# Attention scores over 64 queries of two heads and 192 keys instead of 128 queries of one head and 256 keys

## The chip, the cores and the metric

The kernel runs on one core of a Trainium2 chip. The metric is the device time of one execution in microseconds. A core has a matrix engine (TensorE, "PE" in the profile, with its weight loads as "PEld"), VectorE ("DVE"), ScalarE ("ACT"), GpSimd ("POOL") and SyncE ("SP"), which issues most of the DMAs. Each engine works through its own instructions in order, and semaphores tie the engines together.

## What is computed

One layer of a decoder trunk over 2048 tokens of width 1024, in float32. The input is modulated, u is multiplied with a wide weight matrix, and the result is cut into queries, keys, values, gates and the input of a causal pool. The part that matters here is attention in a window of 128 keys, with 16 query heads of 64 dimensions that share 2 key heads, a bias by distance and one sink logit for each head:

```python
mask = in_window & key_exists            # dist = q_loc + 128 - k_loc, 0 <= dist < 128
logits = einsum('bnqhgd,bnkhd->bnhgqk', qb, kb) * HEAD_DIM ** -0.5 + bias
logits = where(mask, logits, NEG_INF)
probs = softmax(concatenate([logits, sink], -1))[..., :-1]
out = einsum('bnhgqk,bnkhd->bnqhgd', probs, vb)
```

A block of 128 queries meets 256 keys: its own block and the one before. A query at place i of the block sees only the keys i + 1 to i + 128 of these 256. So the first 64 queries of a block see nothing beyond key 191, and the last 64 nothing before key 64.

## The kernel before, in words

Matrices are multiplied as split pairs: each operand is a rounded high part (float32r) and the remainder, and three products (high-high, high-low, low-high) make one. Blocks of four matrices ("quads") are multiplied with seven products instead of eight, after Strassen and Winograd; a product is 12 matmuls of 128x128 weights on 512 columns. The sequence is cut into two halves of 1024 tokens (s = 0, 1). Each half has a start phase, a long phase with 13 single quads in which attention runs beside the products, and an end phase; then come the output phases. `plan` writes the order of products, weight splits and loads ahead of time, and `run` emits them; every operation is kept in program order on its engine. All instructions are recorded by one helper, so the profile gives them all line 56, and they are told apart by tiles.

Attention is the function `overlay`. It has 64 steps a half (8 pairs of heads x 8 blocks of 128 queries). `beat` is called after every three matmuls of a product and now and then emits one `step(n)`, which is software-pipelined over four blocks:

- `scores(n)` on TensorE: four matmuls into the bank `lg`, for each of the two heads one for the high and one for the low part of the keys (tile `kk`); the weights are 128 queries of that head (tile `qs`, high and low parts of the queries one above the other in the 128 rows).
- `transposes(n - 2)`: four 128x128 transposes of the probabilities into the single bank `pt`; `values(n - 3)`: four matmuls into `pv`.
- For step n - 1, VectorE takes the reciprocal of the sums and ScalarE scales the probabilities. ScalarE copies `pt` to `pth` and half of `pv` to `o2`; VectorE later makes the remainder `ptl` and adds the halves into `st`.
- For step n, for each head, VectorE adds the bias tile `bt` to the scores and takes the minimum against the negated sink (one instruction with accumulator), into a tile `L`, and ScalarE takes the exponential with the sum, with the sink as a 257th column.

`L` is a ring of three tiles of 2 x 257 + 4 numbers, and POOL writes the sink columns of the next one (`new_l`). `bt` has one buffer of 2 heads x 256 numbers, reloaded for each pair of heads by `load_bias`. Queries are written to DRAM (`q_d`) by `q_quad` as they are computed, and come back by `load_q` into two buffers of `qs`, two steps at a time. `e_rep` holds the bias rows, repeated for 128 partitions, and `spread_bias` fills it.

A first half's first block has no block before it; its scores are over 128 keys only (`k0_of`).

Score banks: the products of paired quads use the bank `lg` too, and `behind` writes it in full once with a dummy matmul where a phase starts with a fresh bank.

Of the kernel before, what the change touches and what calls it, by code (L numbers as in the profile page):

```python
# [12 lines left out]
F32 = mybir.dt.float32  # L13
F32R = mybir.dt.float32r
# [5 lines left out]
P = 128  # L20
# [39 lines left out]
def kernel(  # L60
# [29 lines left out]

    BF16 = mybir.dt.bfloat16
    set_names = ("B11", "T1", "T2", "B21", "T3", "B22", "T4")

# [53 lines left out]
    def as32(ap):  # L147
        return ap.bitcast(F32)
# [165 lines left out]
    def defer(ticks, f, local=False):  # L314
        due.append((now[0] + ticks, len(due), f, local))
# [136 lines left out]
    def behind(ph, q, kind, h):  # L452
        if kind == "F":
            if h == 0:
                q.c = bank(("lg", "c1")[q.x] if q.pair else "mm")
                if q.x and ph.fresh:
                    t = sets["B11"][:, 0, 0, :]
                    mm(q.c, t[:, 0:P], t, start=True, stop=True, skip_group_check=True)
                    ph.fresh = False
# [88 lines left out]
    def kv_quad(s):  # L548
# [25 lines left out]
        return Quad((win[TK], win[TV]), consume)  # L574

    def q_quad(s, m):
        def consume(ph, mi, t, src):
            hi, lo = ph.c("q_hi", F32R), ph.c("q_lo", F32R)
            act.activation(hi, src, AF.Copy, scale=-0.125)
            dve.scalar_tensor_tensor(lo, src, -0.125, as32(hi), ALU.mult, ALU.subtract)  # L580
            defer(2 if m else 1, lambda: [sp.dma_start(q_d[s, m + mi, t, n], as32(x)) for n, x in enumerate((hi, lo))])
# [184 lines left out]
    def spread_bias(j, q):  # L766
        q.dma_start(e_rep[:, 2 * j : 2 * j + 2, :], e_d[2 * j : 2 * j + 2, :].partition_broadcast(P))

    def overlay(ph, s, n_slots):
# [26 lines left out]
        def load_q(h):  # L796
            if h >= N // 2:
                return
            j, t, c = h // NB, h // 2 % 2, h % 2
            q = qts[h] = tp.tile([P, 2, 2 * P], F32R, tag="qs", bufs=2, name="qs")  # L800
            for n in range(2):
                src = q_d[s, j, t, n][:, c * 2 * P : (c + 1) * 2 * P].rearrange("(h d) c -> d h c", h=2)
                sp.dma_start(as32(q[n * HD : (n + 1) * HD]), src)

        def load_bias(j):
            if j >= KT:
                return
            bt = bts[j] = tp.tile([P, 2, 2 * P], F32, tag="bt", bufs=1, name="bt")
            e_src = e_rep[:, 2 * j : 2 * j + 2, :]
            sp.dma_start(bt, bass.AP(e_src.tensor, e_src.offset + P - 1, [[HEADS * ET - 1, P], [ET, 2], [1, 2 * P]]))  # L810

        def new_l(n):
            if n < N:
                j = n // U
                room = tp.tile([P, 2 * 257 + 4], F32, tag="L", bufs=3, name="L")
                Ls[n] = room[:, 0 : 2 * 257].rearrange("p (h k) -> p h k", h=2)
                marks[n] = room[:, 2 * 257 : 2 * 257 + 2], room[:, 2 * 257 + 2 :]
                pool.tensor_copy(Ls[n][:, :, 256], nsink[:, 2 * j : 2 * j + 2])

# [3 lines left out]
        def values(n):  # L823
            k0 = k0_of(n)
            pv = pvs[n] = bank("pv")[:, 0 : 2 * P].rearrange("p (h q) -> p h q", h=2)
            pair = xs.pop(n)
            todo = [(hf, x) for hf in range(k0 // P, 2) for x in pair]
            for i, (hf, x) in enumerate(todo):
                mm(pv, kvt["v"][:, n % U + hf - 1 + s, :], x[:, hf], start=i == 0, stop=i == len(todo) - 1)

        def scores(n):
            k0, b, q = k0_of(n), n % U, qts[n // 2]
            lg = bank("lg").rearrange("p (h k) -> p h k", h=2)
            at = n % 2 * P
            for h in range(2):
                for hl in range(2):
                    mm(
                        lg[:, h, k0:],
                        q[:, h, at : at + P],
                        kvt["k"][:, hl, (b - 1 + s) * P + k0 : (b + 1 + s) * P],  # L840
                        start=h == 0 and hl == 0,
                        stop=hl == 1,
                        skip_group_check=True,
                    )
            return lg

        def transposes(n):
            L = Ls.pop(n)
            pt = ps.tile([P, 2, 2, P], F32, tag="pt", bufs=1, name="pt")
            for hf in range(k0_of(n) // P, 2):  # L850
                for h in range(2):
                    pe.transpose(pt[:, hf, h, :], L[:, h, hf * P : (hf + 1) * P], ident)
            return pt
# [20 lines left out]
        def step(n):  # L874
# [4 lines left out]
            if n - 1 in Es:  # L879
                E, e0, sm = Es.pop(n - 1)  # L880
                dve.reciprocal(sm, sm)
                for h in range(2):
                    act.activation(E[:, h, e0:256], E[:, h, e0:256], AF.Copy, scale=sm[:, h : h + 1])
            if pt is not None:
# [9 lines left out]
            if lg is not None:  # L894
                j, e0 = n // U, k0_of(n)
                L = Ls[n]
                nm, sm = marks.pop(n)
                for h in range(2):
                    dve.tensor_tensor_reduce(
                        L[:, h, e0:256],  # L900
                        lg[:, h, e0:],
                        bts[j][:, h, e0:],
                        1.0,
                        nsink[:, 2 * j + h : 2 * j + h + 1],
                        ALU.add,
                        ALU.min,
                        nm[:, h : h + 1],
                    )
                    act.activation(
                        L[:, h, e0:257],  # L910
                        L[:, h, e0:257],
                        AF.Exp,
                        bias=nm[:, h : h + 1],
                        scale=-1.0,
                        accum_out=sm[:, h : h + 1],
                    )
                Es[n] = L, e0, sm
            if pt is not None:
                low(dve, lo[:, h0:], pt[:, h0:], hi[:, h0:])
            if o2 is not None:  # L920
# [7 lines left out]
                for h in range(2):  # L928
                    dve.tensor_tensor(
                        outs[jj, tt][h * HD : (h + 1) * HD, bb * P : (bb + 1) * P], pv[0:HD, h, :], o2[:, h, :], ALU.add  # L930
                    )
                if bb == NB - 1:
# [282 lines left out]
    def head(ph, grp):  # L1215
# [402 lines left out]
```

## Time and profile before

| what | value |
|---|---|
| median of three runs | 1698.69 us (1698.04 to 1703.2) |
| the profiled execution | 1703.35 us |
| its span, first to last instruction | 1701.2 us |
| mean granted TensorE clock | 0.993 |
| busy: PE, DVE, ACT, POOL | 98%, 70%, 58%, 35% |
| DMA packets | 236833, 389.50 MB |

The profile is one execution, and its busy shares are of the span. Attention of the first half runs from about 161 to 480 us, that of the second from about 743 to 1060 us. Matmuls are pipelined, so the length of one in the profile is its latency; the time from the start of one to the start of the next tells what it costs in a dense stretch.

### The profile page before, as it was taken

To read this page: it belongs to the slowest core of one execution; us is meant where nothing else is said; L and a number is where in the kernel's file an instruction comes from. 1 tells how busy PE (TensorE), PEld (TensorE's weight loads), DVE (VectorE), ACT (ScalarE), POOL (GpSimd) and SP (SyncE) were. 2 spreads that over 40 slices of the span, in tenths; PEclk is the share of its full clock that TensorE was granted. 3 is DMA by queue.
4 is the path that set the end of the run, shared out by engine and by line. 5 is a ranking of instruction groups with operands and counts; after the bars stand their busy time and mean duration, and the time that the engine had idled before them with its cause. 6 is when DMAs were issued, how large, how long until landed. Compare 5 with 4: busy or idle time off the path is not lost.

```text
span 1701.2 us, 24948 instructions
## 1 busy us (share of the span) xinstructions
PE 1665.3 (98%) x8112; PEld 1397.0 (82%) x8112; DVE 1185.1 (70%) x2167; ACT 988.4 (58%) x1943; POOL 589.4 (35%) x563
## 2 busy tenths in 40 slices
PE   9899999999999999999999999999999999999997
PEld 7788888888788888888888888888888888888886
DVE  6855666666647778656666666487876785778878
ACT  4645888787853336358877787333544453434553
POOL 3013454545462223323424333322242211113544
PEclk9899999999999999999999999999999999999999
DMA  9489676776557889865456454589968685777343
GB/s 358 151 294 311 202 225 217 242 239 208 170 178 223 264 288 326 289 206 157 150 171 215 156 175 135 190 280 326 329 238 309 197 312 201 261 264 281 149 149 124
DMA packets 236833, 389.50 MB, mean 229 GB/s; under 512 B 20872, under 2 KB 90528, under 8 KB 236576
## 3 DMA queue, kind: packets, MB, share of 16 engines
q1 hardware_dynamic: 231280, 382.36, 66.8%
q10 hardware_dynamic: 5392, 5.53, 1.0%
q8 instruction: 64, 1.05, 0.3%
q14 instruction: 65, 0.53, 0.1%
q0 software_dynamic: 32, 0.02, 0.0%
HBM read 243.63 MB, written 147.35 MB: 230 GB/s over the span
## 4 chain that ended last, share of the span: by engine, by line
PE 68%; ACT 11%; DVE 6%; issue 5%; DMA 3%; POOL 1%; SPq 1%; DVEq 0%; ACTq 0%; POOLq 0%
PE mm L56 43%; PE lg L56 11%; PE c L56 9%; ACT L L56 5%; PE pv L56 3%; PE pt L56 3%; DVE w_set L56 2%; ACT pth L56 2%; ACT w_set L56 1%; DVE wide L56 1%; ACT sig L56 1%; DVE p L56 1%; DVE ptl L56 1%; SPq L56 1%; ACT q_hi L56 0%
## 5 line engine op out<-in xcount | busy, mean ns | idle before, releaser
L56 PE MATMUL mm<-set_B,w_set 128*128 128x512 f32 x2664 | 652.7, 391 | 0.6 <-DVE w_set L56 0.6
L56 PEld LDWEIGHTS mm<-set_B,w_set 128*128 128x128 f32 x2664 | 496.6, 188 | 103.7 <-DVE w_set L56 1.5
L56 PE MATMUL mm<-set_T,w_set 128*128 128x512 f32 x1896 | 466.1, 392 | 1.5 <-POOL w_set L56 1.2
L56 POOL TENSOR_TENSOR W<-W 128x512 f32<-128x512 f32 x185 | 266.9, 1453 | 573.1 <-DVE w_set L56 394.0
L56 PEld LDWEIGHTS mm<-set_T,w_set 128*128 128x128 f32 x1896 | 351.5, 189 | 74.4 <-POOL w_set L56 2.5
L56 DVE TENSOR_TENSOR w_set<-W,w_set 128x1024 fp32r<-128x1024 f32 x197 | 254.5, 1292 | 110.5 <-ACT w_set L56 109.2
L56 ACT ACTIVATE L<-L 128x257 f32<-128x257 f32 (+3 forms) x512 | 241.4, 498 | 96.8 <-DVE L L56 96.3
L56 ACT CAST w_set<-W 128x1024 fp32r<-128x1024 f32 x222 | 232.2, 1047 | 97.2 <-PE mm L56 54.2
L56 PE MATMUL lg<-set_T,w_set 128*128 128x512 f32 x828 | 201.0, 391 | 2.7 <-ACT lg L56 1.7
L56 PE MATMUL c<-set_T,w_set 128*128 128x512 f32 x828 | 200.8, 391 | 0.0
L56 PEld LDWEIGHTS lg<-set_T,w_set 128*128 128x128 f32 x828 | 155.4, 188 | 36.2 <-ACT lg L56 2.1
L56 PEld LDWEIGHTS c<-set_T,w_set 128*128 128x128 f32 x828 | 155.8, 189 | 32.2
L56 DVE TENSOR_TENSOR ptl<-pt,pth 128x512 fp32r<-128x512 f32 (+1 forms) x128 | 86.4, 675 | 112.6 <-ACT pth L56 112.6
L56 POOL TENSOR_TENSOR W<-W,A 128x512 f32<-128x512 f32 x41 | 57.9, 1412 | 275.1 <-DMA A<-in_win_dram 102.7
L56 DVE CUSTOM_DVE_ANT_0 L<-lg,bt,nsink 128x256 f32<-128x256 f32 (+1 forms) x256 | 110.1, 467 | 25.1 <-PE lg L56 20.9
L56 ACT ACTIVATE sig<-mm 128x512 f32<-128x512 f32 x76 | 45.5, 599 | 94.6 <-PE mm L56 92.5
L56 PEld LDWEIGHTS lg<-kk,qs 128*128 128x128 f32 x512 | 77.4, 189 | 15.4 <-DVE L L56 4.6
L56 PE MATMUL pt<-ident,L 128*128 128x128 f32 x496 | 76.7, 276 | 9.3 <-DVE ptl L56 8.8
L56 PE MATMUL lg<-kk,qs 128*128 128x256 f32 (+1 forms) x512 | 81.5, 281 | 2.2 <-DVE L L56 1.9
L56 POOL TENSOR_TENSOR w_set<-W,w_set 128x1024 fp32r<-128x1024 f32 x25 | 61.0, 2441 | 63.7 <-ACT w_set L56 37.5
L56 PE MATMUL pv<-pth,vv 128*128 128x256 f32 x248 | 74.8, 323 | 1.1 <-DMA vv<-v_d 1.1
L56 DVE TENSOR_TENSOR st<-pv,o 64x128 f32<-64x128 f32 x256 | 71.3, 279 | 5.5 <-ACT o L56 3.8
(207 smaller groups left out, 1884.2 us busy)
## 6 DMA issues: line engine op xcount, KB each, us to landing
W<-in_win_dram SPq DMA_DIRECT2D x40, 512.0 KB, 5.8
qs<-q_d SPq DMA_DIRECT2D x128, 128.0 KB, 4.3
sums_d<-W SPq DMA_DIRECT2D x62, 256.0 KB, 4.1
W<-sums_d SPq DMA_DIRECT2D x31, 512.0 KB, 4.2
ain_d<-st SPq DMA_DIRECT2D x56, 256.0 KB, 3.5
A<-in_win_dram SPq DMA_DIRECT2D x42, 256.0 KB, 5.6
q_d<-q_hi SPq DMA_DIRECT2D x32, 256.0 KB, 4.4
q_d<-q_lo SPq DMA_DIRECT2D x32, 256.0 KB, 4.2
```

Source lines behind the costliest of these rows:

```text
L56: return lambda *args, **kw: self.tc.keep_in_program_order(op(*args, **kw))
```

## The change

The scores of a step are cut by queries and not by heads. A matmul's weights are now 64 queries of both heads (the first or the last half of the block, index `eo`), and it runs over 192 keys: 0 to 191 for the first half, 64 to 255 for the last. The add-and-minimum, the exponential and the scaling work on the same 192 keys. `L` becomes three standing tiles of 2 x 257 + 14 numbers; the 128 places between the two halves' keys are set to zero once a phase by POOL, so that the transposes still read four 128x128 squares. The sink stands before the keys of the first half and behind those of the last. `bt` holds 64 queries of both heads over 192 places (the bias depends on the distance alone, so both halves share it), has two buffers and takes two DMAs. Queries lie in DRAM in pieces of 64. `nsink` and `sinks` are laid out with the two heads of a pair in the two halves of the partitions. Where an end phase starts, the dummy matmul is done for both banks.

The core of the diff:

```diff
-    nsink = cp.tile([P, HEADS], F32, name="nsink")
+    nsink = cp.tile([P, 2 * KT], F32, name="nsink")[:, :KT]
-    e_rep = dp.tile([P, HEADS, ET], F32, name="e_rep")
+    e_rep = dp.tile([HD, HEADS, ET], F32, name="e_rep")
-    q_d = dp.tile([2, KT, 2, 2, P, CH], F32, name="q_d")
+    q_d = dp.tile([2, KT, 2, 2, CH // HD, P, HD], F32, name="q_d")
...
-            self.fresh = True
+            self.fresh = {0, 1} if "pg" in bufs else {1}
...
-                if q.x and ph.fresh:
+                if q.pair and q.x in ph.fresh:
...
+    def keep_q(dst, x):
+        sp.dma_start(dst.rearrange("b p c -> p b c"), x.rearrange("p (b c) -> p b c", c=HD))
...
+        rooms = [tp.tile([P, 2 * 257 + 14], F32, tag=f"L{i}", bufs=1, name="L") for i in range(3)]
+        for room in rooms:
+            pool.memset(room[:, 1 + BAND : 1 + BAND + P], 0.0)
...
-                src = q_d[s, j, t, n][:, c * 2 * P : (c + 1) * 2 * P].rearrange("(h d) c -> d h c", h=2)
+                src = q_d[s, j, t, n, 4 * c : 4 * c + 4].rearrange("b (h d) c -> d (b h) c", h=2)
...
-            bt = bts[j] = tp.tile([P, 2, 2 * P], F32, tag="bt", bufs=1, name="bt")
+            bt = bts[j] = tp.tile([P, BAND], F32, tag="bt", bufs=2, name="bt")
+            for h in range(2):
...
+        def span_of(n, eo):
+            k0 = k0_of(n)
+            return (max(k0, HD), 2 * P) if eo else (k0, BAND)
...
-            for h in range(2):
+            for eo in range(2):
+                whi = q[:, n % 2 * 2 + eo].rearrange("p h c -> p (h c)")
+                k0, k1 = span_of(n, eo)
                 for hl in range(2):
                     mm(
-                        lg[:, h, k0:],
-                        q[:, h, at : at + P],
-                        kvt["k"][:, hl, (b - 1 + s) * P + k0 : (b + 1 + s) * P],
+                        lg[:, eo, k0:k1],
+                        whi,
+                        kvt["k"][:, hl, (b - 1 + s) * P + k0 : (b - 1 + s) * P + k1],
...
-                    act.activation(E[:, h, e0:256], E[:, h, e0:256], AF.Copy, scale=sm[:, h : h + 1])
+                    x = E[:, 1 + 2 * P * eo + k0 : 1 + 2 * P * eo + k1]
+                    act.activation(x, x, AF.Copy, scale=sm[:, eo : eo + 1])
...
-        act.dma_start(nsink, sinks.partition_broadcast(P))
+        for h in range(2):
+            act.dma_start(nsink[h * HD : (h + 1) * HD, :], sinks[h].partition_broadcast(HD))
...
-        "sinks": a["sinks"][0],
+        "sinks": a["sinks"][0].reshape(-1, 2).T,
```

BAND is 192, P 128, HD 64, KT 8 and CH 512.

More of the change, by code (lines that the diff above doesn't have):

```diff
@@ L580, in consume @@
             dve.scalar_tensor_tensor(lo, src, -0.125, as32(hi), ALU.mult, ALU.subtract)
-            defer(2 if m else 1, lambda: [sp.dma_start(q_d[s, m + mi, t, n], as32(x)) for n, x in enumerate((hi, lo))])
+            defer(2 if m else 1, lambda: [keep_q(q_d[s, m + mi, t, n], as32(x)) for n, x in enumerate((hi, lo))])
         kept = (sums_d[1 + m // 2], s == 1) if m else ()
@@ L847, in transposes @@
         def transposes(n):
-            L = Ls.pop(n)
+            L = Ls.pop(n)[:, 1 : 1 + 4 * P].rearrange("p (e k) -> p e k", e=2)
             pt = ps.tile([P, 2, 2, P], F32, tag="pt", bufs=1, name="pt")
             for hf in range(k0_of(n) // P, 2):
-                for h in range(2):
-                    pe.transpose(pt[:, hf, h, :], L[:, h, hf * P : (hf + 1) * P], ident)
+                for eo in range(2):
+                    pe.transpose(pt[:, hf, eo, :], L[:, eo, hf * P : (hf + 1) * P], ident)
             return pt
@@ L894, in step @@
             if lg is not None:
[L895 to L896 removed]
+                j, L = n // U, Ls[n]
                 nm, sm = marks.pop(n)
[L898 removed]
+                for eo in range(2):
+                    k0, k1 = span_of(n, eo)
+                    a, c = (1 + 2 * P * eo + k for k in (k0, k1))
                     dve.tensor_tensor_reduce(
[L900 to L902 removed]
+                        L[:, a:c],
+                        lg[:, eo, k0:k1],
+                        bts[j][:, k0 - HD * eo : k1 - HD * eo],
                         1.0,
[L904 removed]
+                        nsink[:, j : j + 1],
                         ALU.add,
                         ALU.min,
[L907 removed]
+                        nm[:, eo : eo + 1],
                     )
+                    with_sink = L[:, a : c + 1] if eo else L[:, a - 1 : c]
                     act.activation(
[L910 to L911 removed]
+                        with_sink,
+                        with_sink,
                         AF.Exp,
[L913 removed]
+                        bias=nm[:, eo : eo + 1],
                         scale=-1.0,
[L915 removed]
+                        accum_out=sm[:, eo : eo + 1],
                     )
[L917 removed]
+                Es[n] = L, sm
             if pt is not None:
```

43 lines of the change are left out of this document (22 added, 21 removed).

## The prediction

> **What bounds the kernel now.** I read the page first, then busy time by stage, then what the TensorE waits for, then single bursts in the timeline.
>
> ```profile
> span 1701.2 us, 24948 instructions
> PE 1665.3 (98%) x8112; PEld 1397.0 (82%) x8112; DVE 1185.1 (70%) x2167; ACT 988.4 (58%) x1943; POOL 589.4 (35%) x563
> ...
> PE 68%; ACT 11%; DVE 6%; issue 5%; DMA 3%; POOL 1%; SPq 1%; DVEq 0%; ACTq 0%; POOLq 0%
> ```
>
> The TensorE is busy for 98% of the span, and the chain that ended last runs through it. An engine that gets faster elsewhere is worth only the TensorE idle time that it removes. The change lives in the two attention phases, which the next view separates (us, then PE, PEld, DVE, ACT, POOL busy, clock, DMA share, GB/s):
>
> ```profile
> 150.00:485.00 335.00, 326.38 (x1761) 277.36 (x1760) 209.47 (x603) 266.04 (x650) 163.87 (x182) 0.99 0.69 219
> 485.00:735.00 250.00, 249.24 (x1103) 205.72 (x1103) 178.33 (x244) 108.48 (x156) 90.48 (x71) 1.00 0.79 263
> 735.00:1062.00 327.00, 322.27 (x1771) 276.68 (x1770) 211.33 (x598) 258.26 (x631) 114.70 (x128) 1.00 0.53 171
> ```
>
> Even in the attention phases (first and third row) PE is idle for only 8.6 and 4.7 us. ACT is busy for 79% of both, so the queue of small attention work is what could hold PE up. Who does:
>
> ```profile
> PE pt L56 <- DVE ptl L56: 8.8, 17, 0.7
> ...
> PE lg L56 <- DVE L L56: 1.9, 3, 0.9
> ```
>
> The largest is 8.8 us in 17 waits: the transposes of one step wait until VectorE has emptied the single pt bank of the step before.
>
> **Part 1: the score products.** There are 128 steps, and each issues four score matmuls between 512-column products. 480 of them (120 steps) have 256 columns and become 192; the 8 first blocks have 128 and become 64 and 128.
>
> ```profile
> L56 PE MATMUL lg<-kk,qs 128*128 128x256 f32 x480 | 76.9, 283 | 1.9 <-DVE L L56 1.9
> L56 PE MATMUL lg<-kk,qs 128*128 128x128 f32 x32 | 4.6, 265 | 0.3 <-DMA qs<-q_d 0.3
> L56 PE MATMUL pv<-ct,head_T 128*128 128x1 f32 x32 | 3.8, 247 | 0.2 <-DMA head_T<-in_wadat_dram 0.2
> ```
>
> The means (283, 265) are latencies of pipelined matmuls; what counts is the time from one start to the next. The one-column matmuls of the last row show the floor: 3.8 us over 32 is 0.12 us each, with nothing to stream, so it is the 128x128 weight load that each brings. The timeline has whole bursts of both widths (start, length):
>
> ```profile
> 236.73 0.56 PE L56 MATMUL lg<-kk,qs 128*128 128x128 f32 x4
> 237.12 0.62 PE L56 MATMUL pt<-ident,L 128*128 128x128 f32 x4
> ...
> 238.06 2.24 PE L56 MATMUL mm<-set_T,w_set 128*128 128x512 f32 x9
> ```
> ```profile
> 760.00 0.64 PE L56 MATMUL lg<-kk,qs 128*128 128x256 f32 x4
> 760.47 0.60 PE L56 MATMUL pt<-ident,L 128*128 128x128 f32 x4
> ...
> 761.40 2.95 PE L56 MATMUL mm<-set_T,w_set 128*128 128x512 f32 x12
> ...
> 764.88 0.64 PE L56 MATMUL lg<-kk,qs 128*128 128x256 f32 x4
> ...
> 766.27 2.24 PE L56 MATMUL mm<-set_B,w_set 128*128 128x512 f32 x9
> ```
>
> Four 128-column products take 0.39 us until the transposes start, four 256-column ones 0.47: 0.10 and 0.118 each. The burst up to the next 512-column product takes 1.33 against 1.40 and 1.39. Where does 192 lie? A 512-column product takes 0.227 us (next fence), so a column costs (0.227 - 0.118) / 256 = 0.43 ns, and 192 columns would stream in 0.118 - 64 x 0.43 ns = 0.090 us. That is below the 0.10 us of the 128-column form, so 192 columns sit on the weight-load floor like 128. I take 0.06 us a step: 120 x 0.06 = **7.2 us less**. Ends: 0 (as dear as 256 columns) and 13.1 us (120 x 4 x 64 x 0.43 ns, if streaming alone counted). The 8 first blocks are on the floor already: 0.
>
> [...]
>
> **Part 2: shorter VectorE and ScalarE work.** Each step has two add-and-minimum instructions, two exponentials and two scalings, all over 256 keys, now 192.
>
> ```profile
> L56 ACT ACTIVATE L<-L 128x256 f32<-128x256 f32 x240 | 109.3, 504 | 86.7 <-DVE L L56 86.6
> L56 DVE CUSTOM_DVE_ANT_0 L<-lg,bt,nsink 128x256 f32<-128x256 f32 x240 | 105.2, 475 | 22.8 <-PE lg L56 18.6 <-POOL L L56 3.8
> L56 ACT ACTIVATE L<-L 128x128 f32<-128x128 f32 x16 | 5.6, 397 | 5.1 <-DVE L L56 5.1
> L56 DVE CUSTOM_DVE_ANT_0 L<-lg,bt,nsink 128x128 f32<-128x128 f32 x16 | 4.9, 342 | 2.3 <-PE lg L56 2.3
> ```
>
> Half-way between 504 and 397 ns is 451, so 53 ns less for each of four ACT instructions (25 us of ACT over 120 steps); half-way between 475 and 342 is 408, so 66 ns less for two on DVE (16 us). Nearly all of it lies beside PE work. What reaches the end is the pt wait. One of them, step by step:
>
> ```profile
> 400.32 0.16 DVE L56 RECIPROCAL L<-L 128x2 f32<-128x2 f32 x1
> ...
> 400.58 0.91 ACT L56 ACTIVATE L<-L 128x256 f32<-128x256 f32 x2 [0.89 <-DVE L L56]
> ...
> 401.39 0.56 ACT L56 CAST pth<-pt 128x512 fp32r<-128x512 f32 x1
> ...
> 401.99 0.69 DVE L56 TENSOR_TENSOR ptl<-pt,pth 128x512 fp32r<-128x512 f32 x1 [0.98 <-ACT pth L56]
> ...
> 402.74 0.66 PE L56 MATMUL pt<-ident,L 128*128 128x128 f32 x4 [0.41 <-DVE ptl L56]
> ```
>
> Two scalings stand in front of the copy of pt, so 0.11 us is won for certain; the two exponentials and two adds further ahead can give 0.24 more. Over 17 waits that is 1.8 to 5.8 us; I take 0.2 us each, **3.4 us less**. Ends: 0 (other queued work fills the place) and 8.8. Late next is the same wait, shorter. The values (pv) products and the four transposes keep their sizes, zeros included; the final adds keep 128 elements, in two runs of 64, for which I take 0.
>
> **Part 3: buffers.** L becomes three standing tiles of 2112 bytes in place of a ring of 2072-byte ones. The six POOL memsets of 128 columns are off the path on an engine that is 35% busy; if they hold POOL at the start of a phase until older tiles are free, I bound that at 1 us each, and take 0. bt gets a second buffer, so its load no longer waits for the last reader; it is among the causes of the 17 waits and isn't counted again. Now 512-column products run slower in the attention phase than outside (chain of waits, start, length):
>
> ```profile
> 403.87 3.48 PE mm L56 x15
> ...
> 413.10 2.72 PE mm L56 x12
> ...
> 514.34 2.72 PE mm L56 x12
> ```
>
> 0.232 us each in the first row, 0.227 in the others. If the shifted buffers ended that everywhere, 5 ns over 2184 such products (13 quads of 7 products of 12, twice) would be 11 us; nothing here ties it to addresses, so I take **0.5 us less**, with ends 0 and 6.
>
> **Part 4: the queries through DRAM.** Stores of q go from 128 runs of 2 KB to 1024 of 256 bytes, loads from 128 runs of 1 KB to 512 of 256 bytes.
>
> ```profile
> qs<-q_d SPq DMA_DIRECT2D x128, 128.0 KB, 4.3
> ...
> q_d<-q_hi SPq DMA_DIRECT2D x32, 256.0 KB, 4.4
> ...
> bt<-e_rep SPq DMA_DIRECT2D x16, 256.0 KB, 3.1
> ```
> ```profile
> DMA to landing us min/median/max: 2.6/4.3/8.0
> ```
> ```profile
> q1 hardware_dynamic: 2221, 1.60, 49.8%
> ```
> ```profile
> q1 hardware_dynamic: 317, 0.79, 103.8%
> ```
>
> The fourth line is the landing of the query loads alone. The last two are the queue in 1340 to 1350 us (mean packet 720 bytes) and in 20 to 22 us (2490 bytes): 49.8% of 16 x 10 us over 2221 packets is 36 ns each, 103.8% of 16 x 2 us over 317 is 105 ns. So a packet costs about 8 ns and 0.039 ns a byte, and 256 bytes 18 ns. A store then takes 1024 x 18 / 16 = 1.15 us of the engines against 128 x 88 / 16 = 0.70, a load 0.58 against 0.38: 64 x 0.45 + 128 x 0.2 = 54 us over a span in which they are some 70% busy. It hides as long as the queries come in time:
>
> ```profile
> 399.36 1.35 SPq L56 DMA_DIRECT2D qs<-q_d  x2
> ...
> 407.19 0.64 PE L56 MATMUL lg<-kk,qs 128*128 128x256 f32 x4
> ```
>
> The load issued at 399.36 is for the step at 407.19: 7.8 us of lead, of which 0.7 + 4.3 are used, 2.8 spare. An addition of 0.2 us to 4.3 is covered; with the cover gone, each 1 us too late costs 64 us. At the first step, where PE now waits 0.3 us for qs (row above), I take **0.5 us more**; ends 0 and 2. Sixteen bias loads become 32 of 48 KB, on SP only; the bias rows are spread to 64 partitions, not 128: 0. Two dummy 512-column products are added: 2 x 0.227 = **0.5 us more**. The sinks come by two ACT DMAs in place of one: 0, at most one issue of 0.7 us as in the last fence, and ACT's queue has 0% of the chain.
>
> [...]
>
> **The sum.** -7.2 - 3.4 - 0.5 + 0.5 + 0.5 = -10.1 us. The profiled execution took 1703.35 us (span 1701.2), 4.7 over the median 1698.69 of the three runs, and would become 1693.3; for the median, 1698.7 - 10.1 = **1689 us**.
>
> **The rivals.**
> - The columns are free but the waits refill, or 192 costs like 256 and only the waits shrink: -2.9 to -6.2, so 1692.5 to 1696, no measurable change in most of it. For it: ACT stays 75% busy in those phases, and 13 us of idle is all there is to win. Against: the 128-column burst is shorter in the trace.
> - The streaming counts in full, 13.1 in place of 7.2: 1683. For it: 0.43 ns a column. Against: the 0.12 us of one-column products. [...]
> - Slower: the small packets make the query loads land late. It decides from 7.1 us to landing. At 8.0 us, each of 64 load pairs would be 0.9 us late: +58 - 10, 1746 us. For it: the longest landing is 8.0 already. Against: the median of 4.3.
>
> **How the numbers follow.** Forecast 0.60 (own range 1684 to 1694), no full gain 0.24, streaming 0.08, late queries 0.08. A measurement here can tell about 0.3%, 5.1 us, so faster means below 1693.6. The forecast lies above that in 0.07 of its 0.60, no full gain below it in 0.05 of its 0.24: faster 0.53 + 0.05 + 0.08 = 0.66, same 0.07 + 0.19 = 0.26, slower 0.08. The range leaves out the late queries and a tenth of the rest: 1681 to 1699.
>
> **What would show it.** Four score products until the transposes in about 0.40 us, the burst in 1.33; ACT L near 450 ns, DVE L near 408; the pt wait below 6 us; qs landing under 5.5 us; about 107,000 more packets. Wrong if the score groups stay at 0.47, if PE waits for qs, or if 512-column products change by more than 2 ns.

## The result, and the profile after

The changed kernel took 1689.07 us in the median of four runs (1685.76 to 1690.41), against 1699.76 for the kernel before (four runs beside it): a ratio of 0.9932, 95% interval 0.991 to 0.9954. A second series gave 1687.88 against 1700.1, ratio 0.9923 (0.9909 to 0.9936). The forecast of 1689 us, faster, came true. Its terms did not: the two largest were wrong in opposite directions, so that the nearness of the sum is in part luck.

The page of the profile after, its span, busy time and main DMA queue (packets, MB, share of 16 engines); this execution took 1688.99 us:

```profile
span 1687.2 us, 24759 instructions
...
PE 1657.6 (98%) x8114; PEld 1393.4 (83%) x8114; DVE 1169.1 (69%) x2167; ACT 962.6 (57%) x1943; POOL 592.1 (35%) x569
...
q1 hardware_dynamic: 335600, 378.56, 69.7%
```

Busy time by stage after, in the windows that the prediction used for the kernel before:

```profile
150.00:485.00 335.00, 330.22 (x1804) 282.52 (x1804) 206.94 (x611) 258.19 (x656) 173.69 (x193) 1.00 0.75 217
485.00:735.00 250.00, 248.75 (x1101) 205.21 (x1099) 173.75 (x241) 108.53 (x155) 85.81 (x68) 1.00 0.81 264
735.00:1062.00 327.00, 324.44 (x1799) 279.59 (x1800) 208.95 (x604) 246.88 (x634) 117.49 (x131) 1.00 0.59 171
```

PE is idle for 4.8 and 2.6 us in the two attention phases, where it was 8.6 and 4.7, and the same windows hold more matmuls (1804 against 1761, 1799 against 1771): work that came later has moved up into them.

Where did it move? The row of the score matmuls gives the start of the first and of the last one, which frame both attention phases. Before, then after (duration ns minimum/median/maximum, first and last start in us):

```profile
L56 PE MATMUL lg<-kk,qs x512: 220/281/388, 161.7 to 1049.9; 128*128 128x256 f32 x160, 128*128 128x128 f32 x11
```
```profile
L56 PE MATMUL lg<-kk,qs x512: 192/274/357, 162.6 to 1035.7; 128*128 128x192 f32 x160, 128*128 128x64 f32 x6, 128*128 128x128 f32 x5
```

888.2 us became 873.1: 15.1 us less, between the first and the last score product. Outside, nothing: 161.7 against 162.6 ahead of them, and 651.3 against 651.5 from there to the end of the span. For one figure per version I use below the **stretch**, the time from the start of the 301st to the start of the 3451st matmul on split weights (`w_set`), some 140 to 1060 us: 920.5 before, 905.2 after. The profiled execution before took 1703.35 us, 3.6 above the median of its four, so that 15 us in this pair of profiles stand for some 11 to 12 in the medians.

What PE waits for after (us in total, times, longest):

```profile
PE pt L56 <- DVE ptl L56: 5.3, 14, 0.7
...
PE lg L56 <- DVE L L56: 1.0, 2, 0.5
...
PE lg L56 <- DMA qs<-q_d: 0.5, 2, 0.3
```

The pt wait fell from 8.8 to 5.3 us, close to the 3.4 us that were forecast for it. But the same waits have a second row, that of the weight loads, which the prediction did not read. Before, then after:

```profile
PEld pt L56 <- DVE ptl L56: 14.5, 25, 0.9
PEld lg L56 <- DVE L L56: 4.6, 8, 1.4
```
```profile
PEld pt L56 <- DVE ptl L56: 8.5, 17, 0.9
...
PEld lg L56 <- DVE L L56: 2.1, 3, 0.9
```

The weight load comes ahead of its matmul (in the changed kernel those of the scores start at 395.95 us, the scores at 396.18), so that this row sees a wait from its start, while the matmul's row counts only what is left when the long modelled latency of the matmul before is over (a 512-column product lasts 390 ns in the profile where the next one starts 227 ns after it, both in the median), and leaves waits of a few tenths out. The starts of the matmuls side with the weight loads: from the last matmul ahead of them to the first transpose, the 128 steps together take 13.5 us more than 128 times the median before, and 8.9 us after. The weight loads' rows have 14.5 and 8.5 us, the matmuls' 8.8 and 5.3. By the weight loads 6.0 + 2.5 = 8.5 us went away and not 3.5 + 0.9.

Groups of the narrowed instructions after (busy us, mean ns; then the idle time before them):

```profile
L56 ACT ACTIVATE L<-L 128x192 f32<-128x192 f32 x240 | 96.4, 451 | 88.7 <-DVE L L56 88.4
L56 DVE CUSTOM_DVE_ANT_0 L<-lg,bt,nsink 128x192 f32<-128x192 f32 x240 | 89.2, 410 | 19.8 <-PE lg L56 19.2
```

451 and 410 ns, as interpolated (451 and 408). A whole burst after, in the timeline (start, length):

```profile
746.44 0.59 PE L56 MATMUL lg<-kk,qs 128*128 128x192 f32 x4
746.87 0.60 PE L56 MATMUL pt<-ident,L 128*128 128x128 f32 x4
...
747.78 3.59 PE L56 MATMUL mm<-set_T,w_set 128*128 128x512 f32 x15
```

The score group takes 0.43 us until the transposes, the burst 1.34 until the next 512-column product. Over the 100 bursts of full width the median is 1.342 us, against 1.388 before; over those without a wait, 1.340 against 1.385. That is 0.045 us a step, where 0.06 was taken.

### The profile page after: what moved, and what is told of

Read it like the earlier page. It is cut to its first block, busy times and chain, and to the rows that moved or that the text cites. A ratio compares the mean times of both kernels' runs of the same rounds, so it can differ in the third digit from the quotient of the medians.

```text
span 1687.2 us, 24759 instructions
## 1 busy us (share of the span) xinstructions
PE 1657.6 (98%) x8114; PEld 1393.4 (83%) x8114; DVE 1169.1 (69%) x2167; ACT 962.6 (57%) x1943; POOL 592.1 (35%) x569
## 5 line engine op out<-in xcount | busy, mean ns | idle before, releaser
L56 ACT ACTIVATE L<-L 128x193 f32<-128x193 f32 (+5 forms) x512 | 214.8, 446 | 99.3 <-DVE L L56 98.4
L56 DVE CUSTOM_DVE_ANT_0 L<-lg,bt,nsink 128x192 f32<-128x192 f32 (+2 forms) x256 | 93.6, 404 | 22.9 <-PE lg L56 22.4
L56 PEld LDWEIGHTS lg<-kk,qs 128*128 128x128 f32 x512 | 76.2, 190 | 14.3 <-issue 2.6
L56 PE MATMUL lg<-kk,qs 128*128 128x192 f32 (+2 forms) x512 | 75.9, 270 | 2.0 <-DVE L L56 1.0
L56 POOL TENSOR_TENSOR st<-st,ag 128x512 f32<-128x512 f32 x32 | 46.4, 1451 | 84.3 <-DVE st L56 78.4
L56 ACT CAST pth<-pt 128x512 fp32r<-128x512 f32 (+1 forms) x128 | 71.8, 561 | 7.0 <-PE pv L56 6.1
```

Source lines behind the costliest of these rows:

```text
L56: return lambda *args, **kw: self.tc.keep_in_program_order(op(*args, **kw))
```

## The experiments

All compare with the kernel before, timed beside them. The table has what was measured; the parts below have the edits, the expectations and what follows. A time without a ratio is a single run.

| version | time, us | ratio to before (95%) | stretch, us | PE waits for pt |
|---|---|---|---|---|
| before (profiled 1703.35) | 1699.8 to 1700.9 | 1 | 920.5 | 8.8 in 17 |
| changed | 1687.88 | 0.9923 (0.9909 to 0.9936) | 905.3 | 5.0 in 14 |
| changed, score matmuls wide | 1692.1 | 0.9951 (0.9934 to 0.9968) | 910.4 | 3.1 in 9 |
| before, softmax narrow | 1691.24 | 0.9944 (0.9929 to 0.9958) | 910.4 | 2.9 in 8 |
| changed, 128 keys | 1677.34 | | 895.3 | 1.4 in 3 |
| changed, pt copied first | 1679.4 | 0.9872 (0.9856 to 0.9887) | 897.5 | none |
| before, pt copied first | 1684.37 | 0.9904 (0.9885 to 0.9923) | 905.3 | none |
| pt first, steps 4 beats later | 1684.27 | 0.9898 (0.9877 to 0.992) | 906.2 | none |
| pt first, queries first | 1681.56 | 0.9883 (0.9866 to 0.99) | 896.9 | none |
| changed, queries a step late | 1746.63 | 1.0266 (1.0235 to 1.0297) | 963.3 | 2.6 in 6 |
| changed, stores doubled | 1716.33 | | 925.9 | 4.4 in 11 |
| changed, one bt buffer | 1691.12 | | 905.0 | 4.9 in 13 |
| changed, L tiles as before | 1691.65 | | 908.3 | 5.4 in 13 |

### The changed kernel again

> The changed kernel itself, as a control beside the others. All theories: ratio to before 0.993 (0.991 to 0.9954 so far), burst of twelve small matmuls 1.34 us, pt waits for ptl 5 us in all.

1687.88 us, and a stretch of 905.3 us against 905.2: within the stretch two profiles of the same kernel agree to 0.1 us. The spans differ by 3.6 us (1683.6 and 1687.2), and a difference of that size is there by 82 us, before any attention. That is why stretches are compared below and single times are not, where less than 5 us matters. The agreement is in part chance, since the waits for the first queries alone are 1.6 us in one and 0.5 in the other.

### Score matmuls wide again

```diff
-                k0, k1 = span_of(n, eo)
+                k0, k1 = k0_of(n), 2 * P
```

> The changed kernel with the score matmuls back on 256 columns; VectorE and ScalarE still read 192 of them. Theory (a 192-column product sits on the weight-load floor, and its shorter burst goes straight to the end): burst back from 1.34 to 1.39 us, so about 5.3 us (0.044 x 120 steps) slower than the changed kernel, ratio to before 0.996. Rival (the whole gain is shorter waits behind ScalarE and VectorE): time unchanged, ratio 0.993.

This undoes the narrower score products alone. The timeline (start, length):

```profile
746.28 0.63 PE L56 MATMUL lg<-kk,qs 128*128 128x256 f32 x4
746.76 0.60 PE L56 MATMUL pt<-ident,L 128*128 128x128 f32 x4
...
747.67 3.61 PE L56 MATMUL mm<-set_T,w_set 128*128 128x512 f32 x15
```

0.48 and 1.39 us, as before the change. 4.2 us in the medians and 5.1 in the stretch are lost; the two ratios differ by 0.0028, with an uncertainty of some 0.002, so that the theory (5.3 us) fits and the rival (nothing lost) does not. The narrower products are worth 0.044 x 120 = 5.3 us of PE time. About 2.4 us of that come back as waits, since PE arrives earlier at the next one: beside this version the changed kernel waits 1.9 us more for pt (5.0 against 3.1) and 0.5 more for L. And 2.4 us of the 5.1 go with the first query loads, on which this execution waited 4.0 us and the changed kernel beside it 1.6. So 5.3 - 2.4 + 2.4 = 5.3 us are expected in the stretch, but without the query loads only 2.9 would be.

### The softmax narrow in the kernel before

```diff
+        rooms3 = [tp.tile([P, 2 * 257 + 4], F32, tag=f"L{i}", bufs=1, name="L") for i in range(3)]
+        for room in rooms3:
+            pool.memset(room[:, 0 : 2 * 257].rearrange("p (h k) -> p h k", h=2)[:, :, 0:HD], 0.0)
...
-                room = tp.tile([P, 2 * 257 + 4], F32, tag="L", bufs=3, name="L")
+                room = rooms3[n % 3]
...
-                j, e0 = n // U, k0_of(n)
+                j, e0 = n // U, max(k0_of(n), HD)
```

> The kernel before with only the add-and-minimum, the exponential and the scaling cut to 192 keys (it leaves keys 0 to 63 of each block's 256 out), with three standing L tiles of the old size; score matmuls stay on 256 columns. Theory: burst stays 1.39 us, TensorE waits in the attention phases fall from 21 us to about 12, so 5 to 9 us faster than before, ratio 0.995 to 0.997. Rival (the whole gain is shorter waits): 10 us faster, ratio 0.9935. Second rival (the waits move by chance with the pacing): anything from 0.994 to 1.001, with the pt waits not below 8 us.

The score products stay at 256 columns, queries and bias stay as before; only the adds, exponentials and scalings shrink. L also becomes three standing tiles here; VectorE's waits for POOL's part of L stay as they were (3.8 us before, 4.1 here), so that this is not where the gain comes from. This version brings 8.9 us in the medians, 10.1 in the stretch, 2.6 to 3 times the 3.4 forecast. Its ratio lies between theory and first rival; the second rival falls, since PE's waits for pt go well below 8 us. PE's row for pt:

```profile
PE pt L56 <- DVE ptl L56: 2.9, 8, 0.7
```

So most of the change's gain comes from VectorE and ScalarE, which are 70% and 58% busy, and not from the matmuls on the engine that is 98% busy. The two parts add up, 5.1 + 10.1 = 15.2 of the 15.3 us of the stretch, though the waits for the first queries, 0.3 to 4.0 us in these profiles, make that closer than it need be; in the medians it is 4.2 + 8.9 = 13.1 of 12.2.

### 128 keys for each half

```diff
-            return (max(k0, HD), 2 * P) if eo else (k0, BAND)
+            return (max(k0, P), 2 * P) if eo else (max(k0, HD), BAND)
```

> The changed kernel with scores, exponentials and scalings over 128 keys instead of 192 (it leaves 64 keys of each half-block out). Theory of the weight-load floor: the burst of twelve small matmuls stays at 1.33 to 1.34 us. Rival (columns are streamed at 0.43 ns each): 4 x 64 columns less, 1.23 us. The time also falls with shorter ScalarE and VectorE work, pt waits below 3 us, 1680 to 1686 us.

```profile
752.86 0.56 PE L56 MATMUL lg<-kk,qs 128*128 128x128 f32 x4
753.25 0.63 PE L56 MATMUL pt<-ident,L 128*128 128x128 f32 x4
...
754.19 1.55 PE L56 MATMUL mm<-set_T,w_set 128*128 128x512 f32 x6
```

The burst is 1.33 us: the last 64 columns bring 0.012 us a burst (median 1.330 against 1.342), the 64 before them 0.044 to 0.046. Streaming by the columns would give the same for both. So there is a floor, and 192 columns have nearly reached it. The starts of single matmuls show where it lies: from the second of a group on, score products start 0.119 us apart (median) with 256 columns, 0.112 with 192 and 0.112 with 128, and the one-column matmuls, which also bring weights of their own, 0.112. What the one-column form has in common with the others is a weight load of 128x128; no run changes that load, so that it is not shown to be the cause. Only the time from the first of a group to the second goes on falling with the columns: 0.114, 0.088 and 0.058 us. This run took 1677.34 us, a little less than the 1680 to 1686 expected.

### The copy of pt first

The prediction showed two scalings standing in front of ScalarE's copy of pt. Here the copy goes ahead of them and nothing else moves:

```diff
-                for eo in range(2):
-                    k0, k1 = span_of(n - 1, eo)
-                    x = E[:, 1 + 2 * P * eo + k0 : 1 + 2 * P * eo + k1]
-                    act.activation(x, x, AF.Copy, scale=sm[:, eo : eo + 1])
+                marks_of[n - 1] = E, sm, [[1 + 2 * P * eo + k for k in span_of(n - 1, eo)] for eo in range(2)]
...
+            if n - 1 in marks_of:
+                E, sm, todo = marks_of.pop(n - 1)
+                for eo, (a, c) in enumerate(todo):
+                    act.activation(E[:, a:c], E[:, a:c], AF.Copy, scale=sm[:, eo : eo + 1])
```

> The changed kernel with ScalarE's copy of pt issued ahead of the two scalings instead of behind them. Theory (what is left of the pt waits comes from the scalings standing in front of the copy): pt waits for ptl from 5.3 to under 2.5 us, about 3 us faster than the changed kernel, ratio 0.9915. Rival (the scalings, now later, make the next transposes wait for L, or the wait comes from VectorE's queue and not from ScalarE's): waits for L above 2 us or pt waits unchanged, time the same or up to 3 us slower.

1679.4 us, the fastest of the versions that compute the whole result, 8.5 us below the changed kernel beside it where about 3 were expected. The rival falls: the waits for L do not grow (0.4 us in PE's row, 1.0 in the changed kernel). The timeline of ScalarE and TensorE in the changed kernel, then in the same step of this version (bracket: idle time and what ended it):

```profile
394.95 0.81 ACT L56 ACTIVATE L<-L 128x192 f32<-128x192 f32 x2 [0.89 <-DVE L L56]
395.66 0.56 ACT L56 CAST pth<-pt 128x512 fp32r<-128x512 f32 x1
...
396.18 0.59 PE L56 MATMUL lg<-kk,qs 128*128 128x192 f32 x4
...
397.00 0.42 PEld L56 LDWEIGHTS pt<-ident,L 128*128 128x128 f32 x4 [0.41 <-DVE ptl L56]
397.00 0.66 PE L56 MATMUL pt<-ident,L 128*128 128x128 f32 x4 [0.24 <-DVE ptl L56]
```
```profile
389.57 0.60 ACT L56 CAST pth<-pt 128x512 fp32r<-128x512 f32 x1
...
390.57 0.81 ACT L56 ACTIVATE L<-L 128x192 f32<-128x192 f32 x2 [0.41 <-DVE L L56]
...
392.19 0.59 PE L56 MATMUL lg<-kk,qs 128*128 128x192 f32 x4
...
392.62 0.60 PE L56 MATMUL pt<-ident,L 128*128 128x128 f32 x4
```

In the first, the transposes start 0.82 us behind the scores, in the second 0.43. The difference is 0.39 us: PEld's row says 0.41, PE's 0.24. The waits of the transposes for VectorE are gone, in both rows. What PE still waits for in attention is mainly query loads (3.8 us in 3 waits, at 161, 224 and 728 us; the first and the last are the first load of a phase).

### The same in the kernel before

> The kernel before, full width, with only ScalarE's copy of pt issued ahead of the two scalings. Theory (the shorter softmax of the change is worth time only because it shortens what stands ahead of that copy): pt waits for ptl from 8.8 to under 1.5 us, 12 to 15 us faster than before, ratio 0.991 to 0.993, and only the 5 us of the narrower score products are left between this kernel and the changed one with the same order. Rival (the shorter instructions relieve the queues of ScalarE and VectorE as a whole): the pt waits stay above 4 us, ratio above 0.995.

The edit is that of the last part, on 256 keys. With nothing of the change in it this version takes 1684.37 us, 0.9904, a little more than the 12 to 15 us expected and not slower than the change as a whole, and its stretch is the same as that of the changed kernel, 905.3. The change spent its effect on the length of a queue whose order was the trouble. With both, 920.5 becomes 897.5: the first edit brings 15.2, the second another 7.8. Of the 7.8, 5.3 are the narrower score products again; the rest lies in waits for L (1.6 us here, 0.4 with both) and in one for the values (1.1 us here, none with both). In the medians, from two series, it is 5.0 us, which is what was expected.

### Steps four beats later, with pt first

```diff
-        state = [0, 0.0, 12]
+        state = [0, 0.0, 16]
```

> The changed kernel with the copy of pt first and the first attention step four beats (12 products, 2.7 us) later in each half. Theory (what is left of the TensorE waits are the first query loads of a half, 3.8 us in 3 waits): waits for qs under 1 us, 2 to 3 us faster than with the copy first alone, ratio 0.9855. Rival (the steps that are pushed back crowd at the end of the phase): no gain, ratio 0.987 to 0.988.

```profile
PE lg L56 <- DMA qs<-q_d: 7.5, 3, 3.9
```

A miss: 0.9898 where 0.9855 was expected. The rival's 0.987 to 0.988 lies at the edge of the interval, but the trace shows another cause than the one it named. The waits at the first steps are gone, and two later loads come late instead, by 3.2 and 3.9 us. SP issued these two 3.3 to 3.4 us before PE was ready for them, against 7.4 us in the version without the shift: just ahead of them it had stood for 5.0 and 7.4 us at a load that waited for POOL. They then landed 6.4 and 7.2 us after their issue, where the median is 3.8. Behind both waits PE ran at half clock (behind the first one 0.50 was granted from 247.97 to 251.37 us), and the 512-column products that follow each other take 695.4 us in the stretch, against 689.8 without the shift.

### Queries first, with pt first

```diff
-        load_k(0)
         load_q(0)
+        load_k(0)
```

> The version with ScalarE's copy of pt ahead of the two scalings (1679.4 us, 0.9872 of before), and with the first query load of a phase issued ahead of the first key load. Theory (its remaining 3.8 us of PE waits for qs, at about 160 and 727 us, come from the first query load standing behind the key load on SP): the qs wait falls below 1.5 us, and the time to 1676 to 1679 us, 0.985 to 0.9865. Rival (the first scores need keys as well as queries, and the key load is merely late in its place, or the queries themselves are written late): the wait for qs turns into a wait for kk of the same 2 to 4 us, and the time stays at 1678 to 1681, 0.9865 to 0.988.

1681.56 us against the 1679.4 of the version without it (in another series); the intervals of both ratios overlap. The theory falls, and the rival holds as far as the trace shows it:

```profile
PE lg L56 <- issue: 1.8, 1, 1.8
...
PE lg L56 <- DMA kk<-k_d: 1.2, 1, 1.2
```

The wait for qs turned into one of 1.2 us for kk in the first phase, and in the second one of 1.8 us whose releaser the trace does not show. The first scores need both.

### Query loads one step later

```diff
-            if n < N and n % 2 == 0:
+            if n < N and n % 2 == 1:
```

> The changed kernel with each pair of query loads issued one step (4.7 us) later. By the prediction's working (a lead of 7.8 us, 5 used) the loads then come 1.5 to 2 us late for 60 pairs: PE waits for qs of 90 to 120 us, about 100 us slower, ratio 1.05. Rival (SP runs ahead of the TensorE, so the real lead is 9 to 14 us): under 20 us slower, ratio under 1.005.

```profile
PE lg L56 <- DMA qs<-q_d: 45.5, 18, 6.8
```

The slower rival's mechanism, made to happen: 1746.63 us, 59 more than the changed kernel, between the 100 and the 20 expected. That this is the prediction's own 1746 is chance. Only 18 loads are late, by 2.5 us in the mean, not 64 pairs by 0.9. The lead is uneven, and loads that come late are very late. Half clock behind the long waits adds to it: the mean clock falls from 0.992 to 0.981, and the 512-column products that follow each other take 8.5 us more in the stretch.

### Query stores twice

Each store of the queries is issued a second time, into a tensor that nobody reads.

```diff
+    q_twin = dp.tile([2, KT, 2, 2, CH // HD, P, HD], F32, name="q_twin")
...
-            defer(2 if m else 1, lambda: [keep_q(q_d[s, m + mi, t, n], as32(x)) for n, x in enumerate((hi, lo))])
+            defer(2 if m else 1, lambda: [keep_q(d[s, m + mi, t, n], as32(x)) for d in (q_d, q_twin) for n, x in enumerate((hi, lo))])
```

> The changed kernel with every store of the queries issued twice, the second time into another DRAM tensor that nobody reads: 64 more stores of 1024 runs of 256 bytes, 65,536 more packets and 16.8 MB more. It doubles the price of the stores in small runs by itself. Theory (their packets lie beside other transfers, and SP has time to spare): the stretch from the 301st to the 3451st weight product grows by less than 2 us from 905, the wait of PE for qs stays below 2.5 us in all, and qs lands in a median below 4.6 us. Rival (a store in small runs holds SP for up to 3 us, and the query loads behind it come late): 5 us or more in that stretch, with PE's wait for qs at 4 us or above and SP's longest issue of q_d above 3 us.

My theory fell and the rival holds: 1716.33 us, 20.7 us more in the stretch. The queries land as fast as ever in the median (4.3 us), but PE waits for four of the 64 pairs:

```profile
PE lg L56 <- DMA qs<-q_d: 14.3, 4, 5.5
```

The timeline of SP's issues ahead of the longest of these waits, which PE begins at 399 us:

```profile
390.51 1.16 SPq L56 DMA_DIRECT2D q_d<-q_lo  x1
391.72 1.84 SPq L56 DMA_DIRECT2D q_twin<-q_hi  x1
393.61 0.94 SPq L56 DMA_DIRECT2D q_twin<-q_lo  x1
394.65 1.00 SPq L56 DMA_DIRECT2D ain_d<-st  x1
395.75 1.44 SPq L56 DMA_DIRECT2D W<-in_win_dram  x2
...
397.97 1.30 SPq L56 DMA_DIRECT2D qs<-q_d  x2
...
400.50 1.41 SPq L56 DMA_DIRECT2D qs<-q_d  x2
```

SP goes from issue to issue with 0.10 us or less between them, and the query loads stand at the end of the row. PE waits for the pair issued at 397.97, whose second load lands at 404.69 us, 6.1 us after its issue; PE resumes at 404.82. The second pair of stores here takes 1.84 + 0.94 = 2.8 us of SP ahead of it. The same pair was issued 7.0 us before PE was ready in the changed kernel, and 0.65 us before here. So it is with the two longest waits, 10.4 of the 14.3 us: the loads were issued when PE already stood or nearly so. The two others were issued 5.9 and 4.9 us ahead, a lead that is shorter too, and landed late as well, in 7.7 and 6.8 us. What stores in short runs take from the query loads is mostly SP's issue time; that a few of them also land later is not excluded, since 24 of some 107 landings take more than 6 us here, 17 in the changed kernel and 10 in the one before.

### One buffer for bt, and L tiles of the old size

```diff
-            bt = bts[j] = tp.tile([P, BAND], F32, tag="bt", bufs=2, name="bt")
+            bt = bts[j] = tp.tile([P, BAND], F32, tag="bt", bufs=1, name="bt")
```
```diff
-        rooms = [tp.tile([P, 2 * 257 + 14], F32, tag=f"L{i}", bufs=1, name="L") for i in range(3)]
+        rooms = [tp.tile([P, 2 * 257 + 4], F32, tag=f"L{i}", bufs=1, name="L") for i in range(3)]
```

> The changed kernel with one buffer for the bias tile bt again in place of two; everything else as changed. Theory (the second buffer is worth nothing: the bias load was not among the causes of the 8.8 us of pt waits): the time from the 301st to the 3451st weight product stays at 905 us, within 1 us; the pt wait stays at 5 to 5.5 us in 13 to 15 waits; VectorE's add waits less than 1 us in all for the bias load. Rival (a one-buffer load holds up the first add of each pair of heads): 14 loads of about 3 us, each issued only when the last reader is done, with PE's wait for the scores bank or for pt rising by 2 us or more, and that stretch at 907 us or above.

> The changed kernel with L tiles of 2 x 257 + 4 numbers (2072 bytes a partition) in place of 2 x 257 + 14 (2112 bytes), so that L and what lies behind it start away from multiples of 64 bytes. Theory (addresses tie to nothing here): 512-column products in the attention phases keep their starts 0.226 to 0.232 us apart and sum to 720.6 us within 0.5 us in the stretch from the 301st to the 3451st weight product, which stays at 905 us within 1 us. Rival (the size that keeps wide operands at multiples of 64 bytes is part of the gain): up to 6 us more in that stretch, seen as longer spacing of 512-column products, as longer ScalarE exponentials on L than 451 ns, or as more waits for pt.

The bias buffer is worth nothing (905.0 us). With the old tile size the stretch is 908.3, 3.1 more than with 2112 bytes, which is between theory and rival. 1.8 us of it are one wait for the first queries:

```profile
PE lg L56 <- DMA qs<-q_d: 2.3, 1, 2.3
```

The other part is half clock right behind this wait, granted from 164.8 to 168.2 us, in which five 512-column products start 0.43 to 0.53 us apart. The exponentials stay at 451 to 452 ns, the pt wait at 5.4 us, and 512-column products that start less than 0.3 us apart do so at 0.2288 us in the mean, against 0.2287 in the changed kernel. Waits for the queries lay between 0.3 and 4.0 us in the other versions too, whatever the tile size. So no effect of the addresses is seen.

## Why the prediction was right, and where its steps were wrong

- **The sum**: -10.1 us forecast, -10.7 and -12.2 us measured in two series. Right, but by terms of opposite error.
- **Part 1**, the score products, -7.2: too much. The floor that the 192 columns come near to is shown by the bursts of 1.388, 1.342 and 1.330 us at 256, 192 and 128 columns; that it is the weight load was the author's estimate from the one-column products, and no run shows it. The size was off: the floor was read as 0.10 us from a quarter of 0.39 us, in which the second product of the group follows the first early; between the others it is 0.11 us, so that 256 columns (0.119) stood nearer to it. And the 1.40 of two bursts was 1.388 in the median. 0.044 to 0.046 us x 120 = 5.3 to 5.5 us in place of 7.2; the marker of 0.40 us until the transposes came out as 0.43. After waits that refilled, 4.2 us of it reach the medians. Streaming in full (13.1 us) is excluded: 4 x 64 columns at 0.43 ns, 0.110 us, would have gone from a burst, and 0.046 us did.
- **Part 2**, the shorter softmax, -3.4: far too little; 8.9 us in the medians, 10.1 in the stretch. The step that failed is "Over 17 waits". They were taken from PE's row, 17 and 8.8 us. The weight loads' row has 25 waits for pt and 8 for L, 19.1 us in all. The end of the range given for the term, 8.8, was for the same reason no bound. 0.2 us over those 33 waits would have been 6.6. And in the profiled execution a stall that follows from the waits goes too: after 0.93 and 0.67 us of waiting, just ahead of 454.7 and 456.1 us, the kernel before ran 3.4 us at half clock (below), which cost it 1.6 us. The wait that was read for the term was the right one: its cause, two scalings ahead of the copy of pt, is shown by the two versions that copy first.
- **Part 3**, buffers, -0.5: nothing. 512-column products that start less than 0.3 us apart do so at 0.2287 us in the mean of the stretch, before and after. What made some of them slower is not the layout of L, and stays open.
- **Part 4**, the queries through DRAM, +0.5 at the first load: PE's waits for queries went from 0.3 to 0.5 us in one pair of profiles, and were 1.6 us in the second of the changed kernel, 1.8 and 2.4 in the two versions with the old layout of the queries, so that no effect of the layout is seen. The other +0.5, two dummy products, is there (8114 matmuls against 8112) but was not measured by itself. The transfers cost what was estimated: the DMA share rose from 0.69 to 0.75, from 0.79 to 0.81 and from 0.53 to 0.59 in the three windows, which is 335 x 0.06 + 250 x 0.02 + 327 x 0.06 = 45 us of the 16 engines' time for the change as a whole, against 54 estimated for the queries. The packets of 256 bytes took 18 ns in the median, just as worked out. They did no harm to the median landing of qs, 4.1 us against 4.3 before. The kernel before has 528 packets of 32 to 128 bytes, and those of 128 took 13 ns, which lies on the same line. What the prediction left out is SP's own time, in the last section.
- **The slower rival** was weighed by the wrong quantity. It was to decide at 7.1 us from issue to landing, which was read from the lead of one load. From the issue of the second load of a pair to the time when PE is ready for it, the 64 pairs have 5.3 to 18.4 us before (median 9.5) and 4.2 to 17.3 after; landings of up to 8.0 us before and 7.4 after passed with waits of 0.3 and 0.5 us in all. With the doubled stores it was mainly the issue that came late. "Each 1 us too late costs 64 us" is wrong as well: a few pairs are late by much, and the others not at all.
- **No full gain** (1692.5 to 1696) had half of its mechanism: waits do refill when the products get shorter, by about 2.4 us, but the shorter softmax takes away more than that.

## What to carry to other kernels

Before narrowing the work on an engine, look at the order in its queue: the copy that frees a single matmul bank stood behind two instructions that nobody was in a hurry for, and moving it, without any other edit, brought as much as the whole change. Read waits of a pipelined TensorE at the weight loads, since the matmuls' row hides the part of a wait that lies under the latency of the matmul before (here it has 8.8 us of waits for pt, and the weight loads' row 14.5). When a DMA is cut into shorter runs, count the time that its issue holds the queue (the second query store went from 0.37 to 0.79 us in the median), and who stands behind it.

## What the runs showed of the hardware

**A store in short runs holds the engine that issues it, unevenly.** The rows of the second stores of the queries (`q_lo`), before, after, and the twin of the first one with the stores doubled (ns minimum/median/maximum):

```profile
L56 SPq DMA_DIRECT2D q_d<-q_lo x32: 319/366/1066, 71.0 to 954.6; - x32
```
```profile
L56 SPq DMA_DIRECT2D q_d<-q_lo x32: 359/792/2647, 72.2 to 942.4; - x32
```
```profile
L56 SPq DMA_DIRECT2D q_twin<-q_hi x32: 771/1710/3628, 68.6 to 969.1; - x32
```

The same 256 KB in 1024 runs in place of 128: the first such store takes 0.4 us in the median (`q_hi`, 390 ns before and 396 after), the second 0.8, and with the stores doubled the third 1.7, but the fourth (`q_twin<-q_lo`) 0.8 again. Why they differ was not measured.

**A packet of 256 bytes costs 18 to 19 ns of a DMA engine.** By the packets' own records the 131,072 of the changed kernel take 19.1 ns in the mean, the 196,608 with the stores doubled 18.5, and in both the median is 18. The 18 ns worked out from 720- and 2490-byte packets were right.

**Half clock came in cells of 3.41 us, between 140 and 1062 us behind cells in which PE was idle for 1.60 us or more.** In all 14 traces the granted clock changes only on a grid of 3.41 us, whose place differs from run to run: in the kernel before, up to its last change, it stays at one value for 3.41, 10.24, 30.72, 40.96, 358.40 or 1235.63 us, which is 1, 3, 9, 12, 105 or 362 cells. The version with steps four beats later, two neighbouring cells of its grid (PE, PEld, DVE, ACT, POOL busy, then the granted clock); its wait of 3.15 us lies from 243.9 to 247.05 us:

```profile
244.55:247.96 3.41, 0.91 (x8) 0.94 (x9) 0.20 (x1) 0.00 (x0) 0.00 (x0) 1.00 1.15 296
247.97:251.37 3.40, 3.40 (x11) 2.81 (x10) 1.54 (x7) 2.47 (x9) 0.64 (x1) 0.50 0.16 52
```

and the same of the kernel before:

```profile
453.70:457.11 3.41, 1.81 (x13) 1.51 (x13) 2.14 (x9) 3.08 (x9) 2.81 (x4) 1.00 0.17 64
457.12:460.52 3.40, 3.40 (x11) 2.62 (x10) 1.91 (x7) 2.49 (x7) 0.00 (x0) 0.50 0.84 225
```

In the version with steps four beats later the clock of 0.50 begins 0.92 us after the wait is over, where the next cell begins. In the kernel before, the 512-column products start 0.43 us apart in the cell at 0.50, against 0.227 in the median of the run. Half of 3.41 us is 1.7, so that by estimate the wait of 3.15 us cost 4.8. What goes with half clock in these traces is how long PE was idle within the cell before. Between 140 and 1062 us, 16 cells at full clock are followed by half clock: in 15 of them PE is idle for 1.82 us or more, in the one of the kernel before for 1.60. In the cells that are followed by full clock it is idle for 1.75 us at the most. So half clock did not go by the length of a wait alone: one of 2.04 us in the version with wide score matmuls, at 734 us, is split by a border into 1.04 and 1.00, and the clock stays full; one of 1.82 us with the stores doubled, at 207 us, lies in one cell, and half clock follows.
